# Seven block products in place of eight for 4 of 16 inner tiles of a gate/up projection

## The chip, the cores and the metric

The kernel runs on one core of a Trainium2 chip. Its time is the device time in microseconds; the kernel before takes 2282.24 us (median of 3 runs, 2281.66 to 2282.36).

## The reference

A decoder of two layers for 256 tokens of width 2048, in float32: layer 0 is gated linear attention, layer 1 stick-breaking attention, and behind each comes a SwiGLU feed-forward part of inner width 5632. The change is about the feed-forward part:

```python
def rmsnorm(x, w):
    xf = x.astype(jnp.float32)
    xf = xf * lax.rsqrt(jnp.mean(xf * xf, axis=-1, keepdims=True) + EPS)
    return xf.astype(x.dtype) * w

def swiglu(h, w_gate_up, w_down):
    gate, up = jnp.split(h @ w_gate_up, 2, axis=-1)
    return (jax.nn.silu(gate) * up) @ w_down

h = h + swiglu(rmsnorm(h, ffn_norm_w[layer]), ffn_w_gate_up[layer], ffn_w_down[layer])
```

## The kernel before

Every large product is done at a reduced float32 format of TensorE, with each operand split exactly into a high and a low part, and with three matmuls: high times high, high times low, low times high. `load_w` (L110) streams 128 x 1024 weights into `raw` (pool `wraw`, four buffers), ScalarE casts them to `hi` (L119), and VectorE subtracts to get `lo` (L120), in pool `wsp` of three buffers.

`gemm_tok` (L123) keeps 128 x 128 of the activations stationary and moves 512 columns of weights; for each of the inner tiles `k` and each of the two token tiles `t` it issues the three matmuls of L137. It accumulates in one PSUM bank per token tile, from pool `ps_acc` with four banks; two more pools, `ps_tr` and `ps_x`, have two banks each, for transposes and for the small products of the attention parts.

In `ffn` (L245) the 5632 inner columns are 11 blocks of 512, in three passes of four, four and three. For each block there is a `gemm_tok` over the 16 inner tiles for gate, one for up, and then an evacuation: Silu on ScalarE with the token's reciprocal rms as scale (L258), a product on VectorE (L261), four transposes for each token tile (L264), and the split into `hid_h` and `hid_l` (L267, L268). A pass ends with the down projection of its blocks, `residual_gemm` (L230), which adds to the residual `h` 512 columns at a time (L235).

The activations of a feed-forward part, `xh` and `xl`, are made ahead of it. While the output projection of the attention part runs, `norm_block` (L225) takes each 512 columns of `h` that are done, sums their squares (L202), transposes them (L194) and splits them times the norm's gain (L184, L185). They are not yet divided by the rms. It is known only once all four quarters are summed (`inv_rms`, with a power on POOL at L211), and is multiplied in by the evacuations, L258 and L261.

The transposed activations lie in pool `xt`, two buffers of 32 KB per partition; a feed-forward part uses one of them for `xh` and `xl`.

The order of the instructions on each engine isn't that of the text. A scheduler goes through them once, when the kernel is built, with the text's order as priority and a modelled time for each; each engine's queue is then fixed. A tile of a pool can be filled again once the last reader of the buffer is done.

Of the kernel before, what the change touches and what calls it, by code (L numbers as in the profile page):

```python
# [8 lines left out]
F32 = mybir.dt.float32  # L9
F32R = mybir.dt.float32r  # L10
# [28 lines left out]
PASSES = ((0, 1, 2, 3), (4, 5, 6, 7), (8, 9, 10))  # L39


@with_exitstack
def trunk_kernel(
# [67 lines left out]
    def load_w(ap, k0, nk, c0, ncol, dst=None):  # L111
# [7 lines left out]
        a.copy(hi[:, :n], raw[:, :n])  # L119
        v.tensor_tensor(lo[:, :n], raw[:, :n], hi.bitcast(F32)[:, :n], ALU.subtract)  # L120
# [21 lines left out]
    def gemm_tok_in_turn(w_ap, kt, lhs, c0, evac, k_row0):  # L142
        """gemm_tok with the block of weights held, so that the first token tile is done before the second."""
# [13 lines left out]
    def gemm_col(w_ap, c0, nct, xhl, dst, scale):  # L157
        """dst[column, 256 tokens] for nct column tiles from c0, times scale: weights stationary, activations moving."""
# [45 lines left out]
    def inv_rms(ss, n, name):  # L204
        """ss [P, NT, parts] -> (sum / n + eps) ** -0.5, [P, NT]"""
# [8 lines left out]
    def along_tokens(r, name):  # L214
        """r [token, NT] -> [P, 256], the same row on every partition."""
# [14 lines left out]
    def residual_gemm(w_ap, kt, lhs, k_row0, after=None, after_tile=None):  # L230
        """h += lhs @ w, 512 columns at a time."""
# [13 lines left out]
    def ffn(layer, xh, xl, r, **after):  # L245
        w_gu, w_dn = ffn_w_gate_up[layer], ffn_w_down[layer]
        lhs = lambda k, t: (xh[:, k, t * P : (t + 1) * P], xl[:, k, t * P : (t + 1) * P])
        with tc.tile_pool(name=f"ffn{layer}", bufs=2) as fp:
            for blocks in PASSES:
                hid = []  # L250
                for b in blocks:
# [3 lines left out]
                    sg = [fp.tile([P, NB], F32, name="sg", bufs=4) for _ in range(NT)]  # L255

                    def evac_gate(t, acc, sg=sg):
# [339 lines left out]
```

## Time and profile before

| | |
|---|---|
| median of the runs | 2282.24 us |
| profiled execution, first to last instruction (span) | 2279.7 us |
| what the median has beyond the span | 2.5 us |
| TensorE busy | 2263.7 us, 99% |
| VectorE busy | 1238.5 us, 54% |
| ScalarE busy | 1046.4 us, 46% |
| mean granted TensorE clock | 0.999 of full speed |

The profile is of one execution, and its own time is the span. Busy time of TensorE overlaps from one matmul to the next: a matmul has 0.39 us on its row and the next one begins before it ends, so what a matmul costs is read from the distance of starts. PE is TensorE's matmuls, PEld its weight loads, DVE is VectorE, ACT is ScalarE, SP the queue that issues the loads.

### The profile page before, as it was taken

The numbers are of one execution on the slowest core, as the hardware profiler recorded it, in microseconds if no ns is written. First come the engines' busy times: TensorE is split into PE (matmuls) and PEld (weight loads), VectorE is DVE, ScalarE is ACT, GpSimd is POOL, SyncE is SP. The second block draws the span as 40 slices with busy tenths as digits, with TensorE's granted clock in tenths as the row PEclk, the third lists the DMA queues.
The fourth block names the chain that finished last, engine by engine and source line by source line (L and its number), as shares of the span: only waits on it lengthen the run. The fifth ranks groups of instructions, "written<-read, shape, count | busy, mean of one in ns | idle before, by whom it ended". The sixth has DMA issues, their size and how long they took to land.

```text
span 2279.7 us, 27154 instructions
## 1 busy us (share of the span) xinstructions
PE 2263.7 (99%) x10658; PEld 1891.0 (83%) x10658; DVE 1238.5 (54%) x1251; ACT 1046.4 (46%) x1222; POOL 60.4 (3%) x72
## 2 busy tenths in 40 slices
PE   9999999999999999999999999999999999999998
PEld 7888878888888888888888888888888888888887
DVE  6766455545545545544664567655445444554555
ACT  6544444444434443344554446554444344434444
POOL 2100000000000000000000111000000000000000
PEclk9999999999999999999999999999999999999999
DMA  7554555666666666666566654556666666666664
GB/s 224 169 164 143 153 166 181 188 188 190 188 193 193 189 189 193 194 186 193 185 186 194 186 185 141 167 184 191 186 192 190 193 190 192 186 194 193 191 188 157
DMA packets 242712, 419.23 MB, mean 184 GB/s; under 512 B 12972, under 2 KB 64264, under 8 KB 242456
## 3 DMA queue, kind: packets, MB, share of 16 engines
q1 hardware_dynamic: 242408, 416.44, 60.5%
q8 instruction: 83, 1.36, 0.2%
q10 hardware_dynamic: 176, 1.06, 0.1%
q14 instruction: 45, 0.37, 0.0%
HBM read 415.35 MB, written 2.10 MB: 183 GB/s over the span
## 4 chain that ended last, share of the span: by engine, by line
PE 99%; DVE 0%; issue 0%; DMA 0%; ACT 0%; SPq 0%; POOLq 0%; POOL 0%; DVEq 0%; ACTq 0%
PE acc L137 82%; PE acc L169 7%; PE acc L170 4%; PE px L397 1%; PE tr L264 1%; PE tr L194 1%; PE acc L172 0%; PE acc L154 0%; PE px L494 0%; PE tr L525 0%; PE px L439 0%; DMA raw<-in_gla_w_in_dram 0%; DVE B L356 0%; PE px L409 0%; PE tr L526 0%
## 5 line engine op out<-in xcount | busy, mean ns | idle before, releaser
L120 DVE TENSOR_TENSOR lo<-raw,hi 128x1024 fp32r<-128x1024 f32 (+1 forms) x783 | 972.1, 1243 | 938.4 <-ACT hi L119 937.9
L119 ACT CAST hi<-raw 128x1024 fp32r<-128x1024 f32 (+1 forms) x783 | 823.7, 1052 | 1043.1 <-PE acc L137 904.3
L137 PE MATMUL acc<-hi,xhl 128*128 128x512 f32 x4096 | 1274.7, 391 | 0.8 <-ACT xhl L184 0.8
L137 PEld LDWEIGHTS acc<-hi,xhl 128*128 128x128 f32 x4096 | 769.4, 188 | 161.1 <-issue 1.9
L137 PE MATMUL acc<-lo,xhl 128*128 128x512 f32 x2048 | 799.9, 391 | 0.0
L137 PEld LDWEIGHTS acc<-lo,xhl 128*128 128x128 f32 x2048 | 385.1, 188 | 78.7
L137 PE MATMUL acc<-lo,hid_h 128*128 128x512 f32 x680 | 264.9, 390 | 0.0
L137 PE MATMUL acc<-hi,hid_l 128*128 128x512 f32 x680 | 264.6, 389 | 0.0
L169 PE MATMUL acc<-xhl,hi 128*128 128x512 f32 x735 | 256.1, 396 | 0.6 <-ACT hi L119 0.6
L137 PE MATMUL acc<-hi,hid_h 128*128 128x512 f32 x680 | 240.7, 390 | 0.0
L170 PE MATMUL acc<-xhl,lo 128*128 128x256 f32 x784 | 209.6, 281 | 2.1 <-DVE lo L120 2.0
L169 PEld LDWEIGHTS acc<-xhl,hi 128*128 128x128 f32 x735 | 134.8, 188 | 27.7 <-ACT hi L119 1.0
L170 PEld LDWEIGHTS acc<-xhl,lo 128*128 128x128 f32 x784 | 147.7, 189 | 8.8 <-DVE lo L120 3.0
L137 PEld LDWEIGHTS acc<-hi,hid_l 128*128 128x128 f32 x680 | 127.7, 188 | 26.5
L137 PEld LDWEIGHTS acc<-hi,hid_h 128*128 128x128 f32 x680 | 127.6, 188 | 26.3
L137 PEld LDWEIGHTS acc<-lo,hid_h 128*128 128x128 f32 x680 | 127.6, 188 | 26.1
L184 ACT ACTIVATE xhl<-tr,gains 128x256 fp32r<-128x256 f32 x96 | 40.9, 470 | 28.2 <-PE tr L194 20.9
L185 DVE SCALAR_TENSOR_TENSOR xhl<-tr,gains,xhl 128x256 fp32r<-128x256 f32 x96 | 42.4, 478 | 13.0 <-ACT xhl L184 13.0
L235 DVE TENSOR_TENSOR h<-acc,h 128x512 f32<-128x512 f32 x64 | 41.2, 682 | 7.6 <-PE acc L154 5.2
L258 ACT ACTIVATE sg<-acc,n_r 128x512 f32<-128x512 f32 x44 | 30.0, 690 | 20.8 <-PE acc L137 20.8
L267 ACT CAST hid_h<-tr 128x512 fp32r<-128x512 f32 x44 | 23.6, 589 | 31.4 <-PE tr L264 31.4
L268 DVE TENSOR_TENSOR hid_l<-tr,hid_h 128x512 fp32r<-128x512 f32 x44 | 28.3, 686 | 17.3 <-ACT hid_h L267 17.3
(153 smaller groups left out, 709.1 us busy)
## 6 DMA issues: line engine op xcount, KB each, us to landing
raw<-in_ffn_w_gate_up_dram SPq DMA_DIRECT2D x352, 512.0 KB, 3.9
raw<-in_ffn_w_down_dram SPq DMA_DIRECT2D x176, 512.0 KB, 3.7
raw<-in_gla_w_in_dram SPq DMA_DIRECT2D x97, 512.0 KB, 3.9
raw<-in_sb_w_kv_dram SPq DMA_DIRECT2D x64, 512.0 KB, 3.9
raw<-in_gla_w_out_dram SPq DMA_DIRECT2D x32, 512.0 KB, 3.7
raw<-in_sb_w_q_dram SPq DMA_DIRECT2D x32, 512.0 KB, 3.6
raw<-in_sb_w_out_dram SPq DMA_DIRECT2D x32, 512.0 KB, 3.7
h<-in_x_dram SPq DMA_DIRECT2D x8, 256.0 KB, 5.7
```

The costliest lines, as they stand in the source:

```text
L119: a.copy(hi[:, :n], raw[:, :n])
L120: v.tensor_tensor(lo[:, :n], raw[:, :n], hi.bitcast(F32)[:, :n], ALU.subtract)
L137: pe.matmul(acc[t], l, r[:, j, :], start=(k == 0 and n == 0), stop=(k == kt - 1 and n == 2))
L169: pe.matmul(acc[c], hi[:, j, cs], both, start=first, stop=False)
L170: pe.matmul(acc[c][:, :S], lo[:, j, cs], xhl[:, k0 + j, 0, :], start=False, stop=False)
L184: a.mul(dst_h, src, scale)
L185: v.scalar_tensor_tensor(dst_l, src, scale, dst_h.bitcast(F32), ALU.mult, ALU.subtract)
L194: pe.transpose(tp[:, o : o + P], src(t)[:, j * P : (j + 1) * P], ident)
L235: v.tensor_tensor(hs, acc, hs, ALU.add)
L258: a.activation(sg[t], acc, AF.Silu, scale=r[:, t : t + 1])
L267: a.copy(hh[:, :, ts], tv)
L268: v.tensor_tensor(hl[:, :, ts], tv, hh.bitcast(F32)[:, :, ts], ALU.subtract)
```

## The change

Four of the 16 inner tiles are taken as two pairs. For a pair, the two inner tiles, the two token tiles and the two column halves (gate, up) make a 2 x 2 by 2 x 2 block product. Done plainly it has eight block products; here it has seven, on sums and differences of blocks (Winograd's form of Strassen's scheme). The sums mix the two token tiles, so the tokens have to be divided by their rms ahead.

- `normed_xt`, at the start of `ffn`, replaces `norm_block` ahead of the two feed-forward parts: it waits for the rms, scales `h` by it (ScalarE, 512 columns and one token tile at a time), transposes and splits all four quarters, and forms and splits the sums of the token tiles for the two pairs. The output projection is followed only by the sums of squares (`sums`).
- Block 0 of each layer is done plainly (`eight`), with gate and up side by side. The ten others are done by `seven`: first four products M1, M5, M6, M7 over both pairs into four PSUM banks, then the recombination of the banks by ScalarE and VectorE, and then the three other products of each pair, onto the recombined banks, with two plain inner tiles behind each pair, and then the rest of the twelve plain tiles.
- The differences of weights are formed by VectorE in `room`, which is the second buffer of pool `xt`. They are split in a pool with two buffers (`pair(..., fp, bufs=2)`).
- A weight load takes one inner tile of gate and up together, where it took two inner tiles of one.
- `ps_acc` has six banks and `ps_x` is gone; its users take banks from `ps_acc`.
- The evacuations have no scale.

The diff, cut to its core:

```diff
+XS = 2
-    ps_acc = ctx.enter_context(tc.tile_pool(name="ps_acc", bufs=4, space=PSUM))
+    ps_acc = ctx.enter_context(tc.tile_pool(name="ps_acc", bufs=6, space=PSUM))
-    ps_x = ctx.enter_context(tc.tile_pool(name="ps_x", bufs=2, space=PSUM))
+    def split(hi, lo, src):
+        a.copy(hi, src)
+        v.tensor_tensor(lo, src, hi.bitcast(F32), ALU.subtract)
+    def three(acc, x, w, start, stop, onto=False):
+        (xh, xl), (wh, wl) = x, w
+        for n, (l, r) in enumerate(((xh, wh), (xh, wl), (xl, wh))):
+            pe.matmul(acc, l, r, start=start and n == 0, stop=stop and n == 2, skip_group_check=onto)
+    def normed_xt(ss, key, sums):
+        xh, xl, _ = xt_pair()
+        sh, sl = sums
+        r = inv_rms(ss, D, "n")
...
+        for nb in range(NCB):
+            hs = []
+            for t in range(NT):
+                n = stat.tile([P, NB], F32, name="junk")
+                a.mul(n, h[:, t, nb * NB : (nb + 1) * NB], r[:, t : t + 1])
+                hs.append(n)
+            make_xt(lambda t: hs[t], nb, [(key, 0, xh, xl)])
+        for i in range(XS):
+            q = stat.tile([P, 2, S], F32, name="junk")
+            v.tensor_tensor(q, xh.bitcast(F32)[:, 2 * i : 2 * i + 2, :], xl.bitcast(F32)[:, 2 * i : 2 * i + 2, :], ALU.add)
+            a11, a12, a21, a22 = (q[:, k, t * P : (t + 1) * P] for t in (0, 1) for k in (0, 1))
+            f = stat.tile([P, 4, P], F32, name="junk")
+            v.tensor_tensor(f[:, 0, :], a21, a22, ALU.add)
+            v.tensor_tensor(f[:, 1, :], f[:, 0, :], a11, ALU.subtract)
+            v.tensor_tensor(f[:, 2, :], a11, a21, ALU.subtract)
+            v.tensor_tensor(f[:, 3, :], a12, f[:, 1, :], ALU.subtract)
+            split(sh[:, i], sl[:, i], f)
+        return xh, xl
...
+            room = xt_pair()[2].bitcast(F32).rearrange("p k s c -> p (k s c)").rearrange("p (n c) -> p n c", c=NB)
...
+            def pair(src, pool, **kw):
+                hi, lo = (pool.tile([P, 1024], F32R, name=n, **kw).rearrange("p (k c) -> p k c", k=2) for n in ("hi", "lo"))
+                n = src.shape[1]
+                split(hi[:, :n], lo[:, :n], src)
+                return [(hi[:, j, :], lo[:, j, :]) for j in range(n)]
+            def plain(acc, b, k, start, stop, onto=False):
+                raw = wraw.tile([P, 1024], F32, name="raw").rearrange("p (k c) -> p k c", k=2)
+                load(raw, b, k)
+                for c, w in enumerate(pair(raw, wsp)):
+                    for t in range(NT):
+                        three(acc[t][c], lhs(k, t), w, start, stop, onto)
+            def seven(b):
+                m1, m5, m6, m7 = (ps_acc.tile([P, NB], F32, name="acc") for _ in range(4))
+                held = []
+                for i in range(XS):
+                    first, last = i == 0, i == XS - 1
+                    w3 = room[:, 3 * (i % 2) : 3 * (i % 2) + 3, :]
+                    t32 = room[:, 6 + 2 * (i % 2) : 8 + 2 * (i % 2), :]
+                    w2 = room[:, 10 + 3 * i : 13 + 3 * i, :]
+                    load(w3[:, 0:2, :], b, 2 * i)
+                    load(w2[:, 0:2, :], b, 2 * i + 1)
+                    v.tensor_tensor(w3[:, 2, :], w3[:, 1, :], w3[:, 0, :], ALU.subtract)
+                    b11, t1 = pair(w3[:, 0::2, :], fp, bufs=2)
+                    v.tensor_tensor(t32, w2[:, 1:2, :].broadcast_to([P, 2, NB]), w3[:, 1:3, :], ALU.subtract)
+                    v.tensor_tensor(w2[:, 2, :], w2[:, 0, :], t32[:, 1, :], ALU.subtract)
+                    t3, t2 = pair(t32, fp, bufs=2)
+                    three(m1, lhs(2 * i, 0), b11, first, last)
+                    three(m5, summed(i, 1), t1, first, last)
+                    three(m6, summed(i, 2), t2, first, last)
+                    three(m7, summed(i, 3), t3, first, last)
+                    held.append(w2)
+                p1, p5, u2 = (fp.tile([P, NB], F32, name="part", bufs=3) for _ in range(3))
+                a.copy(p1, m1)
+                a.copy(p5, m5)
+                v.tensor_tensor(u2, m6, p1, ALU.add)
+                v.tensor_tensor(m6, u2, p5, ALU.add)
+                v.tensor_tensor(m7, m7, u2, ALU.add)
+                v.tensor_tensor(m5, m7, p5, ALU.add)
+                acc = ((m1, m6), (m7, m5))
+                todo = list(range(2 * XS, KD))
+                for i, w2 in enumerate(held):
+                    b21, b22 = pair(w2[:, 0:2, :], wsp)
+                    (t4,) = pair(w2[:, 2:3, :], wsp)
+                    three(m1, lhs(2 * i + 1, 0), b21, False, False, True)
+                    three(m6, summed(i, 4), b22, False, False, True)
+                    three(m7, lhs(2 * i + 1, 1), t4, False, False, True)
+                    for _ in range(2):
+                        plain(acc, b, todo.pop(0), False, False, True)
...
+                    acc = seven(b) if b else eight(b)
+                    for t, (gate, up) in enumerate(acc):
+                        sg = fp.tile([P, NB], F32, name="sg", bufs=3)
+                        a.activation(sg, gate, AF.Silu)
+                        v.tensor_tensor(sg, up, sg, ALU.mult)
...
-    residual_gemm(gla_w_out[0], KD, lhs_of(oh, ol), 0, lambda nb, ss=ss: norm_block(ss, nb, [("ffn0", 0, fh, fl)]))
-    r1 = inv_rms(ss, D, "n")
+    residual_gemm(gla_w_out[0], KD, lhs_of(oh, ol), 0, sums(ss))
+    ffn(0, ss, "ffn0", after=to_kqv)
```

## Rows read from the trace of the kernel before

**Rows 1.** Part 1 of the page: busy us (share of the span) xinstructions of each engine.

```profile
PE 2263.7 (99%) x10658; PEld 1891.0 (83%) x10658; DVE 1238.5 (54%) x1251; ACT 1046.4 (46%) x1222; POOL 60.4 (3%) x72
```

**Rows 2.** Part 4: the chain of waits that ended last, shares by engine.

```profile
PE 99%; DVE 0%; issue 0%; DMA 0%; ACT 0%; SPq 0%; POOLq 0%; POOL 0%; DVEq 0%; ACTq 0%
```

**Rows 3.** That chain in order of time, two gate/up blocks: start, us, what.

```profile
474.98 43.54 PE acc L137 x192
519.39 43.54 PE acc L137 x192
```

**Rows 4.** TensorE's waits, two of five: line <- releaser: us, times, longest.

```profile
PE tr L104 <- POOL mf L327: 3.8, 1, 3.8
...
PE acc L170 <- DVE lo L120: 2.0, 1, 2.0
```

**Rows 5.** Waits of VectorE and ScalarE, the largest of each.

```profile
DVE lo L120 <- ACT hi L119: 937.9, 732, 3.3
...
ACT hi L119 <- PE acc L137: 904.3, 553, 3.8
```

**Rows 6.** Busy us of PE, PEld, DVE, ACT, POOL in one block; PEclk, DMA share, GB/s.

```profile
475.20:519.60 44.40, 44.40 (x202) 36.85 (x201) 22.21 (x20) 19.19 (x21) 0.00 (x0) 1.00 0.64 190
```

**Rows 7.** Timeline, output projection to layer 0's first gate tiles: start, us, engine, line, operation.

```profile
424.47 1.28 DVE L235 TENSOR_TENSOR h<-acc,h 128x512 f32<-128x512 f32 x2
...
424.53 0.84 PE L137 MATMUL acc<-hi,xhl 128*128 128x512 f32 x3
...
427.72 0.69 POOL L211 TENSOR_TENSOR n_r<-n_s,neg_half 128x2 f32<-128x2 f32 x1 [87.07 <-DVE n_s L209]
...
429.52 0.38 PE L194 MATMUL tr<-ident,h 128*128 128x128 f32 x2
...
429.98 0.82 PE L194 MATMUL tr<-ident,h 128*128 128x128 f32 x6
...
430.50 0.84 ACT L184 ACTIVATE xhl<-tr,gains 128x256 fp32r<-128x256 f32 x2 [1.73 <-PE tr L194]
```

**Rows 8.** Groups by line and shape: xcount | busy us, mean ns | idle before.

```profile
L120 DVE TENSOR_TENSOR lo<-raw,hi 128x1024 fp32r<-128x1024 f32 x781 | 970.7, 1244 | 935.7 <-ACT hi L119 935.2
...
L119 ACT CAST hi<-raw 128x1024 fp32r<-128x1024 f32 x781 | 822.4, 1053 | 1042.5 <-PE acc L137 904.3 <-PE acc L169 98.8 <-ACT xhl L184 17.1
...
L551 DVE TENSOR_TENSOR h<-h,fw 128x512 f32<-128x512 f32 x6 | 3.9, 686 | 0.2 <-ACT junk L202 0.2
...
L484 ACT ACTIVATE vv<-acc,n_r 128x512 f32<-128x512 f32 x8 | 5.4, 690 | 4.0 <-PE acc L137 4.0
...
L558 ACT ACTIVATE h<-h,y_r 128x512 f32<-128x512 f32 x2 | 1.4, 723 | 2.1 <-POOL y_r L211 2.1
...
L268 DVE TENSOR_TENSOR hid_l<-tr,hid_h 128x512 fp32r<-128x512 f32 x44 | 28.3, 686 | 17.3 <-ACT hid_h L267 17.3
```

**Rows 9.** Windows (columns of rows 6) with and behind idle TensorE.

```profile
66.00:70.00 4.00, 2.03 (x13) 1.46 (x12) 4.00 (x7) 1.67 (x3) 0.00 (x0) 1.00 0.03 11
...
2270.00:2272.00 2.00, 1.32 (x6) 0.75 (x4) 0.64 (x1) 0.00 (x0) 0.00 (x0) 1.00 0.28 109
...
2274.00:2276.00 2.00, 0.00 (x0) 0.00 (x0) 1.45 (x3) 0.63 (x1) 0.00 (x0) 1.00 0.37 139
...
2276.00:2278.00 2.00, 0.00 (x0) 0.00 (x0) 0.00 (x0) 0.00 (x0) 0.00 (x0) 0.65 1.02 381
```

**Rows 10.** Timeline at the end of a gate/up block.

```profile
513.30 1.41 DVE L261 SCALAR_TENSOR_TENSOR sg<-acc,n_r,sg 128x512 f32<-128x512 f32 x2
...
518.36 1.03 PE L264 MATMUL tr<-ident,sg 128*128 128x128 f32 x8
...
519.61 1.29 DVE L268 TENSOR_TENSOR hid_l<-tr,hid_h 128x512 fp32r<-128x512 f32 x2 [0.79 <-ACT hid_h L267]
```

**Rows 11.** Timeline of TensorE around its wait for a low part.

```profile
67.02 0.63 PE L169 MATMUL acc<-xhl,hi 128*128 128x512 f32 x2
69.61 0.50 PE L170 MATMUL acc<-xhl,lo 128*128 128x256 f32 x2 [1.97 <-DVE lo L120]
```

More of the change, by code (lines that the diff above doesn't have):

```diff
@@ new lines, in ffn, with load, eight @@
+    def ffn(layer, ss, key, **after):
+        w_gu, w_dn = ffn_w_gate_up[layer].rearrange("k (g c) -> k g c", g=2), ffn_w_down[layer]
+        with tc.tile_pool(name=f"ffn{layer}", bufs=2) as fp:
+            sh, sl = (fp.tile([P, XS, 4, P], F32R, name=n, bufs=1) for n in ("sum_h", "sum_l"))
+            xh, xl = normed_xt(ss, key, (sh, sl))
+            lhs = lambda k, t: (xh[:, k, t * P : (t + 1) * P], xl[:, k, t * P : (t + 1) * P])
+            summed = lambda i, n: (sh[:, i, n - 1, :], sl[:, i, n - 1, :])
+            room = xt_pair()[2].bitcast(F32).rearrange("p k s c -> p (k s c)").rearrange("p (n c) -> p n c", c=NB)
+            def load(dst, b, k):
+                nc.sync.dma_start(dst, w_gu[k * P : (k + 1) * P, :, b * NB : (b + 1) * NB])
+            def pair(src, pool, **kw):
[46 more added lines that the diff above has]
+                        plain(acc, b, todo.pop(0), False, False, True)
+                while todo:
+                    k = todo.pop(0)
+                    plain(acc, b, k, False, not todo, True)
+                return acc
+            def eight(b):
+                acc = [[ps_acc.tile([P, NB], F32, name="acc") for _ in (0, 1)] for _ in range(NT)]
+                for k in range(KD):
+                    plain(acc, b, k, k == 0, k == KD - 1)
+                return acc
@@ L342, in trunk_kernel @@
         for k0 in range(0, GKT, 2):
-            up = ps_x.tile([P, 512], F32, name="px")
+            up = ps_acc.tile([P, 512], F32, name="acc")
             for j in (0, 1):
@@ L384, in level @@
             if m == P:
-                sp = ps_x.tile([P, 512], F32, name="px")
+                sp = ps_acc.tile([P, 512], F32, name="acc")
                 for hd in range(GH):
@@ L391, in level @@
             if m:
-                sp = ps_x.tile([P, 512], F32, name="px")
+                sp = ps_acc.tile([P, 512], F32, name="acc")
                 for x8 in range(GH * NT):
@@ L404, in level @@
             for h0 in (0, 2):
-                sp = ps_x.tile([P, 512], F32, name="px")
+                sp = ps_acc.tile([P, 512], F32, name="acc")
                 for x4 in range(4):
@@ L447, in trunk_kernel, with sums, after, to_kqv @@
     lhs_of = lambda xh, xl: (lambda k, t: (xh[:, k, t * P : (t + 1) * P], xl[:, k, t * P : (t + 1) * P]))
-    fh, fl, _ = xt_pair()
-    ss = stat.tile([P, NT, NCB], F32, name="ss")
-    residual_gemm(gla_w_out[0], KD, lhs_of(oh, ol), 0, lambda nb, ss=ss: norm_block(ss, nb, [("ffn0", 0, fh, fl)]))
-    r1 = inv_rms(ss, D, "n")
-    kh, kl, khl = xt_pair()
-    qh, ql, qhl = xt_pair()
-    ss = stat.tile([P, NT, NCB], F32, name="ss")
-    ffn(0, fh, fl, r1, after=lambda nb, ss=ss: norm_block(ss, nb, [("kv", 0, kh, kl), ("attn1", 0, qh, ql)]))
+    def sums(ss):
+        def after(nb):
+            for t in range(NT):
+                sumsq(ss[:, t, nb : nb + 1], h[:, t, nb * NB : (nb + 1) * NB])
+        return after
+    ss = stat.tile([P, NT, NCB], F32, name="ss")
+    residual_gemm(gla_w_out[0], KD, lhs_of(oh, ol), 0, sums(ss))
+    kqv = []
+    def to_kqv(nb):
+        if not kqv:
+            kqv.extend((xt_pair(), xt_pair(), stat.tile([P, NT, NCB], F32, name="ss")))
+        (kh, kl, _), (qh, ql, _), ss = kqv
+        norm_block(ss, nb, [("kv", 0, kh, kl), ("attn1", 0, qh, ql)])
+    ffn(0, ss, "ffn0", after=to_kqv)
+    (kh, kl, khl), (qh, ql, qhl), ss = kqv
     r2 = inv_rms(ss, D, "n")
@@ L534, in trunk_kernel @@
             attend(pr, qp)
-    fh, fl, _ = xt_pair()
-    ss = stat.tile([P, NT, NCB], F32, name="ss")
-    residual_gemm(sb_w_out[0], KD, lhs_of(oh, ol), 0, lambda nb, ss=ss: norm_block(ss, nb, [("ffn1", 0, fh, fl)]))
-    r3 = inv_rms(ss, D, "n")
+    sf = stat.tile([P, NT, NCB], F32, name="ss")
+    residual_gemm(sb_w_out[0], KD, lhs_of(oh, ol), 0, sums(sf))
     ss = stat.tile([P, NT, NCB], F32, name="ss")
```

27 lines of the change are left out of this document (8 added, 19 removed).

## The prediction

> **What bounds the kernel now.** The page's first part comes first: TensorE is busy 99% of the span, VectorE 54%, ScalarE 46% [rows 1]. A busy TensorE need not be its peak, so the chain that ended last is next: 99% of it is TensorE [rows 2]. In order of time that chain shows the gate/up blocks as unbroken runs of 192 matmuls in 43.54 us, so one 512-column matmul takes 43.54 / 192 = 0.2268 us, and the next run begins 44.41 us after the last [rows 3]; the 0.87 us between are eight transposes. The waits say whether anything feeds it late: TensorE's waits are five rows, 7.5 us in all, of which the two largest are shown [rows 4]. The other side waits for TensorE: ScalarE's weight cast stands 904 us for matmuls, and VectorE's subtraction follows the cast [rows 5]. So matmuls taken out of gate/up are worth their 0.2268 us, as long as the two engines that split the weights keep up. In one gate/up block they are busy 22.2 and 19.2 us of 44.4 [rows 6].
>
> **The matmuls removed.** A block has 16 inner tiles x 2 token tiles x 2 (gate, up) x 3 (split products) = 192 matmuls. In a seven-product block four inner tiles are taken in two pairs; a pair needs 7 products in place of 8, 3 matmuls each, so 6 fewer per block. Ten of a layer's 11 blocks are changed: 2 x 10 x 6 = 120 matmuls, 120 x 0.2268 = 27.2 us off the path. Everything else has to stay under that.
>
> **The start of each feed-forward layer.** Now the transposes of the residual need no scale, so three quarters of them lie beside the output projection and the last 512 columns beside the first gate tiles. After the change the tokens are divided first, so no transpose can begin before the last square is summed. The chain from the trace of layer 0 [rows 7]: the projection's last matmul is the first of the three that begin at 424.53, so TensorE's next slot is 424.76. The residual add of both token tiles ends at 425.75, the squares, the reduction and the scalar follow, and the POOL power ends at 427.72 + 0.69 = 428.41. All that is there today, under matmuls. New behind it: two ScalarE scalings (0.72 each by the scaling from SBUF, 0.69 by that from PSUM [rows 8]) to 429.85; four transposes, half of the 1.03 for eight [rows 10], to 430.4; the first split (0.84 for two, so 0.42) to 430.85; and the first gate matmul at about 430.95. The hole is 430.95 - 424.76 = 6.2 us, less 0.87 for eight transposes that are in the stream today: 5.3 us, and twice that is 10.6 us. If fewer casts stand between, 4.5 each; if two casts of 1.05 get in, 7.4. The other three quarters are covered by block 0, which stays with eight products: each asks ScalarE for 2 x 0.72 + 4 x 0.42 + 4 casts x 1.05 = 7.3 us in the 10.9 us of its 48 matmuls.
>
> **The clock in that hole.** This trace has two stretches to compare. Ahead of 69.6 TensorE stood for 2 us [rows 11] and the granted clock stayed at 1.00, its 2.4 GHz level; after its last matmul, which ended at about 2271.3, it was still 1.00 up to 2276 and 0.65 on average over the next 2 us, so (0.6 us at 1.00, 1.4 at 0.50) it fell to the 1.2 GHz level at about 2276.6, 5.3 us after [rows 9]. A hole of 6.2 us with four transposes late in it lies at that edge. I take 0.5 us per layer, 1 us in all; the ends are 0 and 3.1 per layer (as long at half speed as the hole was, 6.2 us of which half is lost). The Trainium skill speaks against this edit: "TensorE: Matmul & The Clock Gate", section "Why this matters for your kernels", asks for no long idle gaps between bursts of matmuls, since one puts the array back to its half clock. By the rule the upper end is due, by the row at 67 us nothing; it is a rival below.
>
> **The first part of a seven-product block.** Per pair VectorE makes three differences (0.69 + 1.24 + 0.69 by the rows for 512 and 1024 columns in rows 8) and two subtractions for the split (2 x 1.24): 5.1 us, against 12 matmuls of 2.72 us. The differences need only loaded weights and their own room, free since early in the block before, so they lie under that block, where VectorE is half idle. The splits can't go so far ahead: their pool holds two buffers, and the first pair takes both. With the block's first matmul at 0: the buffer with B11 and T1 is last read by the sixth matmul, which ends at 5 x 0.2268 + 0.39 = 1.52; cast 1.05 and subtraction 1.24 [rows 8] make the low part ready at 3.9, and TensorE wants it at 2.95. A hole of 0.95. What fills it: the high-part matmul of the next product, 0.23, and the eight transposes of the block before, 0.87, which today stand 3.7 us after that block's last evacuation [rows 10], just where the hole is. That the order is made by readiness and not by the text is seen where two high-part matmuls stand ahead of a low part that is late [rows 11]. In 16 blocks 1.10 of filling covers 0.95; in the four that open a pass behind a down projection (blocks 4 and 8) there are no such transposes, and 0.72 stays open. The second buffer's split (ready at about 5.2) is in time.
>
> **The recombination.** VectorE needs two operations (0.69 each, by the subtraction from PSUM in rows 8) behind M6's last matmul before M6's bank can be added to, 1.4 us, plus the matmul's 0.39. Meanwhile TensorE has M7 (0.68), the product on M1 (0.68) and the first plain tile's part on M1 (0.68): 2.04 us. Covered, if taken in this order. The two copies on ScalarE end earlier.
>
> **What crowds VectorE.** In the ten microseconds from the end of a block it has the two gate times up (1.4), one plain subtraction (1.24), two of the pair (2.5), two for the hidden tile (1.37) and the four of the recombination (2.75): 9.3 us, so an awkward order costs. For the block: 22.2 + 5.2 (differences) + 3.9 (two and two half subtractions more) + 2.7 = 34 us of 43; ScalarE 19.2 + 4.7 = 24. I take 0.4 us per block for 16 and 0.75 for four, 9.4 us in all. The ends: 0, and 1.9 (the hole of 0.95 unfilled, and as much again when the recombination waits behind both hidden subtractions), 38 us over 20 blocks.
>
> **Edits put at nothing.** The evacuations without scale are no longer than today's. The sums of token tiles, some 3 us of VectorE per pair, lie under block 0. Loads move the same bytes in the same 512 KB, and DMA is at 0.64 there [rows 6]. One PSUM pool of six in place of four and two: outside the feed-forward TensorE waits under 4 us for what could change, so within 3 us either way.
>
> **Sum.** -27.2 + 10.6 + 1.0 + 9.4 = -6.2 us on the profiled span of 2279.7, so 2273.5; the median of the runs is 2282.24, 2.5 above that span, so 2276.0.
>
> **Rivals.**
> (a) The first part fills completely: no stall in a block, start holes of 4.5: -27.2 + 9 = -18, 2264. For it: TensorE hardly waits anywhere today. Against: VectorE has never been asked for 34 of 43 us in the part of the trace that shows blocks.
> (b) The other side: the two buffers of the pair's splits decide. Place: the second pair and the recombination of each changed block. The point from which it decides is a stall of (27.2 - 11.6) / 20 = 0.78 us a block. Price at 1.5 us a block: -27.2 + 11.6 + 30 = +14.4, 2297. For it: 5.1 us of VectorE against 2.72, and a hole of 0.95 that something else must fill. Against: the filling is there in 16 of 20 blocks.
> (c) The first layer's order is worse: all 32 transposes ahead of the first gate matmul. Then the hole grows by three quarters of 2 x 0.72 + 4 x 0.42 = 3.1 us, about 9.4 a layer: -6.2 + 18.8 = +12.6, 2295. Against: transposes and matmuls mix in twos and sixes in today's order [rows 7].
> (d) The half clock: it falls in both holes and costs 3.1 each: -6.2 - 1 + 6.2 = -1, 2281. For it: the fall at the end of the trace, and the rule named above. Against: transposes come inside the hole.
> (e) That the product count doesn't matter, because the splits set the pace: ScalarE's 904 us of waiting for matmuls excludes it for plain tiles; for the changed part it is (b).
>
> **How the numbers follow.** About 0.2%, 4.6 us, can be told from no change. Forecast (2268 to 2282): 0.42; (a) 0.15; (b) 0.25; (c) 0.08; (d) 0.10. Faster by more: all of (a), 0.35 of the forecast's and 0.03 of (d), so 0.53. Within: 0.07 of the forecast, 0.07 of (d), 0.04 of (b) at its lower edge, so 0.18. Slower: the rest of (b), and (c), 0.29. The range goes from (a) to beyond (b) at 1.5 us a block: 2264 to 2300; the forecast's own is 2268 to 2282.
>
> **What would show it.** TensorE's matmuls fall by 120. After each output projection a hole of about 6 us with squares, POOL power and scalings in it, and the granted clock there says whether (d) holds. From run to run a block takes 43.05 us plus its stall, in place of 44.41; the waits of TensorE for VectorE's low part and for the banks of the recombination give that stall, and over 0.78 us a block decides for (b). VectorE's busy time should rise by about 20 x 11.8 = 236 us. The prediction is wrong if blocks are no shorter than 44.4 us, or if the holes are over 8 us.

## The result: 4.2% slower, and the profile after

The changed kernel takes 2376.6 us (2373.9 to 2384.1) beside 2281.9 for the one before: ratio 1.042, 95% interval 1.0404 to 1.0437. Forecast were 2276.0 and a range of 2264 to 2300, so sign and range were both wrong. Ratios leave out disturbed executions; there is one, of the four of e2 below, at 5058.7 us, without which e2's median would be 2343.3 and not 2344.1. Parts 1 and 4 of its page answer to [rows 1, 2]:

```profile
PE 2288.5 (96%) x10538; PEld 1878.5 (79%) x10538; DVE 1448.8 (61%) x1555; ACT 1131.7 (48%) x1362; POOL 54.6 (2%) x72
...
PE 80%; DVE 9%; DMA 6%; issue 2%; ACT 1%; POOL 1%; SPq 0%; DVEq 0%; POOLq 0%; ACTq 0%
```

The 120 matmuls are gone, and VectorE's busy time rose by 210 us, where 236 were forecast. Yet TensorE, 99% of the chain before, is 80% of it now, and VectorE has 9% with an average load of only 61%. TensorE's waits (line, releaser: us in total, times, longest) stand against 7.5 us in five rows before [rows 4]:

```profile
PE acc L253 <- DVE lo L113: 26.1, 35, 1.2
PE acc L604 <- POOL qp L180: 11.1, 8, 2.3
PE acc L253 <- DVE acc L331: 9.8, 6, 2.2
PE tr L198 <- ACT junk L265: 8.6, 2, 4.3
PE acc L488 <- DVE lev L480: 4.6, 1, 4.6
PE acc L253 <- ACT hi L112: 4.4, 11, 1.1
...
PE acc L447 <- POOL gl L180: 3.6, 1, 3.6
```

Three places can be read off. L253 is gate/up (low parts, recombination). L604, L488 and L447 are not in the feed-forward at all: attention, the scores and the log decay of layer 0. L198 is the start of each feed-forward layer. By the last residual additions of each stage, the span grew by 9.1 us up to the first output projection, 35.8 and 34.7 in the two feed-forward layers and 17.4 in attention.

One seven-product block (columns as in [rows 6]) took 46.5 us, not 43.05 plus a little, with VectorE at 32 us, close to the 34 forecast:

```profile
820.00:866.50 46.50, 44.56 (x196) 35.33 (x195) 31.97 (x35) 22.88 (x27) 0.00 (x0) 1.00 0.60 181
```

Of the 3.45 us beyond 43.05, TensorE was idle for 1.94 (46.50 - 44.56). The rest lies in its busy time, where matmuls begin further apart; so the rows of waits show less than what the stops cost. VectorE is not full in a block; it is full at the handover from one block to the next. VectorE's timeline there (start, us, line, operation; in brackets the idle time before and what ended it):

```profile
772.19 1.23 DVE L319 TENSOR_TENSOR xhl<-xhl 128x1024 f32<-128x1024 f32 x1 [1.36 <-DMA xhl<-in_ffn_w_gate_up_dram]
773.33 0.68 DVE L365 TENSOR_TENSOR sg<-acc,sg 128x512 f32<-128x512 f32 x1
773.93 1.22 DVE L113 TENSOR_TENSOR lo<-raw,hi 128x1024 fp32r<-128x1024 f32 x1
775.06 0.69 DVE L320 TENSOR_TENSOR xhl<-xhl 128x512 f32<-128x512 f32 x1
775.66 0.69 DVE L330 TENSOR_TENSOR part<-acc,part 128x512 f32<-128x512 f32 x1
776.26 1.22 DVE L113 TENSOR_TENSOR lo<-xhl,hi 128x1024 fp32r<-128x1024 f32 x1
777.39 0.70 DVE L331 TENSOR_TENSOR acc<-part 128x512 f32<-128x512 f32 x1
778.00 0.70 DVE L332 TENSOR_TENSOR acc<-acc,part 128x512 f32<-128x512 f32 x1
```

From 772.19 to 786.2 VectorE has no idle time. L319 and L320 are differences of the second pair. The first of them waited 1.36 us for its load, and the gate times up (L365) stood behind it in VectorE's queue. In the chain of waits (start, us, what) that load begins when a subtraction of a held tile of the block before ends:

```profile
766.16 1.24 DVE lo L113
767.41 4.75 DMA xhl<-in_ffn_w_gate_up_dram
```

Over the whole run VectorE stood 58.3 us for loads ahead of a difference (13.5 ahead of L317, 44.8 ahead of L319). The two differences then stand ahead of the plain low part, the recombination (L330 to L333) and the low parts of held tiles. TensorE's timeline in the same stretch stops for those:

```profile
775.20 0.50 PE L253 MATMUL acc<-lo,xhl 128*128 128x512 f32 x1 [0.21 <-DVE lo L113]
...
777.53 0.50 PE L253 MATMUL acc<-lo,xhl 128*128 128x512 f32 x1 [1.14 <-DVE lo L113]
...
780.81 1.36 PE L253 MATMUL acc<-hi,xhl 128*128 128x512 f32 x3 [0.21 <-ACT hi L112]
```

### The profile page after: what moved, and what is told of

Same layout as the page of the kernel before. It is cut to its first block, busy times and chain, and to the rows that moved or that the text cites. A ratio compares the mean times of both kernels' runs of the same rounds, so it can differ in the third digit from the quotient of the medians.

```text
span 2376.7 us, 27301 instructions
## 1 busy us (share of the span) xinstructions
PE 2288.5 (96%) x10538; PEld 1878.5 (79%) x10538; DVE 1448.8 (61%) x1555; ACT 1131.7 (48%) x1362; POOL 54.6 (2%) x72
## 4 chain that ended last, share of the span: by engine, by line
PE 80%; DVE 9%; DMA 6%; issue 2%; ACT 1%; POOL 1%; SPq 0%; DVEq 0%; POOLq 0%; ACTq 0%
PE acc L141 36%; PE acc L253 28%; PE acc L173 7%; DMA xhl<-in_ffn_w_gate_up_dram 6%; DVE lo L113 5%; PE acc L174 4%; PE acc L497 1%; ACT hi L112 1%; PE tr L198 1%; DVE hid_l L113 1%; DVE part L330 0%; PE acc L604 0%; POOL qp L180 0%; DVE xhl L320 0%; PE acc L176 0%
## 5 line engine op out<-in xcount | busy, mean ns | idle before, releaser
L113 DVE TENSOR_TENSOR lo<-raw,hi 128x1024 fp32r<-128x1024 f32 (+1 forms) x703 | 874.8, 1246 | 700.5 <-ACT hi L112 699.9
L112 ACT CAST hi<-raw 128x1024 fp32r<-128x1024 f32 (+1 forms) x703 | 735.3, 1049 | 870.6 <-PE acc L141 424.7
L253 PE MATMUL acc<-hi,xhl 128*128 128x512 f32 x2416 | 775.4, 396 | 6.2 <-ACT hi L112 4.4
L253 PEld LDWEIGHTS acc<-hi,xhl 128*128 128x128 f32 x2416 | 457.4, 190 | 114.2 <-ACT hi L112 13.4
L253 PE MATMUL acc<-lo,xhl 128*128 128x512 f32 x1208 | 478.9, 397 | 26.1 <-DVE lo L113 25.6
L141 PE MATMUL acc<-hi,xhl 128*128 128x512 f32 x1280 | 402.7, 393 | 0.9 <-ACT xhl L188 0.9
L253 PEld LDWEIGHTS acc<-lo,xhl 128*128 128x128 f32 x1208 | 229.2, 190 | 86.9 <-DVE lo L113 41.1
L141 PEld LDWEIGHTS acc<-hi,xhl 128*128 128x128 f32 x1280 | 240.5, 188 | 52.3 <-issue 1.7
L141 PE MATMUL acc<-lo,xhl 128*128 128x512 f32 x640 | 251.7, 394 | 0.0
L112 ACT CAST hi<-xhl 128x1024 fp32r<-128x1024 f32 (+1 forms) x160 | 149.5, 945 | 181.6 <-PE acc L253 156.1
L113 DVE TENSOR_TENSOR lo<-xhl,hi 128x1024 fp32r<-128x1024 f32 (+1 forms) x160 | 172.2, 1089 | 50.9 <-ACT hi L112 50.6
L141 PEld LDWEIGHTS acc<-lo,xhl 128*128 128x128 f32 x640 | 120.5, 188 | 26.3 <-issue 1.9
```

Source lines behind the costliest of these rows:

```text
L112: a.copy(hi, src)
L113: v.tensor_tensor(lo, src, hi.bitcast(F32), ALU.subtract)
L141: pe.matmul(acc[t], l, r[:, j, :], start=(k == 0 and n == 0), stop=(k == kt - 1 and n == 2))
L253: pe.matmul(acc, l, r, start=start and n == 0, stop=stop and n == 2, skip_group_check=onto)
```

## Experiments: which part costs what

All times are medians, and the kernel before took 2281.8 to 2282.0 beside each. The theory, from the waits above: the shared PSUM pool costs 26.5 us, the divided tokens 16 to 20, and the rest is stalls in seven-product blocks. The rivals were the prediction's own sizes and, for e4, the new shape of a block.

**e1_one_pool**: the kernel before with the pools alone changed.

```diff
-    ps_acc = ctx.enter_context(tc.tile_pool(name="ps_acc", bufs=4, space=PSUM))
-    ps_x = ctx.enter_context(tc.tile_pool(name="ps_x", bufs=2, space=PSUM))
+    ps_acc = ctx.enter_context(tc.tile_pool(name="ps_acc", bufs=6, space=PSUM))
...
-            za = ps_x.tile([P, 512], F32, name="px")
+            za = ps_acc.tile([P, 512], F32, name="acc")
```

> The kernel before with one edit: PSUM pool of six banks that the small products of the two attention parts share, in place of four and two. Theory: the 9.1 us that the GLA part and the 17.4 us that the attention part of layer 1 are longer in the changed kernel's trace come from the shared pool alone, so 2282 + 26.5 = 2308 us, with the feed-forward parts as long as before (732 and 722 us). Rival, as the prediction put it: the pool is worth at most 3 us either way, so 2279 to 2285, and the two parts are longer in the changed kernel because the scheduler's order there is moved by the feed-forward parts next to them.

2315.4, ratio 1.0148 (1.0132 to 1.0163): +33.6, where the theory had 26.5 and the rival at most 3. The same waits as in the changed kernel appear in a kernel with nothing else changed:

```profile
PE acc L493 <- POOL qp L175: 13.0, 8, 2.3
PE acc L387 <- DVE lev L379: 4.6, 1, 4.6
...
PE acc L346 <- POOL gl L175: 3.6, 1, 3.6
```

L493 is a score's matmul that waits until POOL has scaled the queries, once for each of the eight pairs of heads. Before, it took its bank from a pool of its own, and the next pair's query product ran meanwhile.

**e2_scoped**: the changed kernel with banks 4+2 outside the feed-forward and 6 in it.

```diff
+    share(0, 4, 2)
...
+    share(1, 6, 0)
     ffn(0, ss, "ffn0", after=to_kqv)
+    share(2, 4, 2)
...
-            za = ps_acc.tile([P, 512], F32, name="acc")
+            za = banks["x"].tile([P, 512], F32, name="px")
```

> The changed kernel with its PSUM split by part: four and two banks in the GLA and attention parts as before, six in the feed-forward parts as in the change. Theory (the pool costs 26.5 us outside the feed-forward parts): 2376.6 - 26.5 = 2350 us, GLA and attention parts back to 424.5 and 386 us. Rival (the pool is not it): 2374 to 2379 us.

2344.1, ratio 1.0265 (1.0248 to 1.0282): 32.5 less than the changed kernel. The pool's price is nearly the same added (33.6) or taken away.

**e11_text_order**: e1 with the next pair's query product written ahead of the scores.

```diff
-            attend(pr, qp)
+            if ahead is not None:
+                attend(pr - 1, ahead)
+            ahead = qp
+        attend(SH // 2 - 1, ahead)
```

> The kernel with one PSUM pool of six and nothing else changed (2315.35 us), with the text of the attention part in another order: the query product of the next pair of heads is written ahead of the attention of this pair. Theory F (a pool hands out its banks in the order of the text, so the next query product gets no bank until the scores of this pair have theirs, and these wait for POOL's scaling): the attention part goes from 406 to 386 to 390 us, 2296 to 2300 us. Rival (six shared banks are simply too few for both): it stays over 400 us, 2310 to 2320.

2299.1, ratio 1.0075 (1.0061 to 1.0089): 16.2 of the 33.6 come back, and layer 1's attention takes 386.7 us beside 385.9 before and 405.7 in e1. So in layer 1 the price is one of order: one pool gave its banks out in the order of the text, and the next query product stood behind the scores in it. The rest is in layer 0, where the text was left as it was.

**e3_normed**: the kernel before with the tokens divided ahead of their split.

```diff
+                a.mul(n, h[:, t, nb * NB : (nb + 1) * NB], r[:, t : t + 1])
...
-                        a.activation(sg[t], acc, AF.Silu, scale=r[:, t : t + 1])
+                        a.activation(sg[t], acc, AF.Silu)
```

> The kernel before with one edit: the tokens are divided by their rms ahead of transposing and splitting, at the start of each feed-forward part; blocks, products and PSUM as before. Theory from the changed kernel's trace (TensorE stands 6.5 us, of which 0.87 is transposes that stood there before, and the next nine matmuls are 0.43 us apart in place of 0.23, so 2.5 us with the transposes at the same rate): 2 x 8.2 = 16 us, so 2298 us. Rival, the prediction's own term: 2 x 5.8 = 11.6 us, so 2293.5. Second rival: the later quarters also stall TensorE (block 0 ended 9.9 us later in the changed kernel, not 8.2): 20 us, 2302.

2297.0, ratio 1.0066 (1.0049 to 1.0083): +15.2, where the prediction had 11.6. TensorE's timeline in the changed kernel at the start of layer 0's feed-forward answers to [rows 7]:

```profile
433.69 0.39 PE L141 MATMUL acc<-hi,xhl 128*128 128x512 f32 x1
438.37 2.16 PE L198 MATMUL tr<-ident,junk 128*128 128x128 f32 x8 [4.29 <-ACT junk L265]
440.45 0.80 PE L253 MATMUL acc<-hi,xhl 128*128 128x512 f32 x1
...
444.03 1.46 PE L253 MATMUL acc<-hi,xhl 128*128 128x512 f32 x5
```

and the windows of its end and of what follows to [rows 9]:

```profile
438.00:441.00 3.00, 2.63 (x9) 1.94 (x10) 0.48 (x1) 1.99 (x4) 0.00 (x0) 0.50 0.93 324
441.00:444.00 3.00, 3.00 (x8) 2.32 (x7) 1.96 (x4) 2.22 (x6) 0.00 (x0) 0.50 1.00 356
```

The hole is 440.45 - 433.92 = 6.5 us, where 6.2 were forecast. But behind it the granted clock is 0.50, the 1.2 GHz level: eight matmuls take 444.03 - 440.45 = 3.58 us in place of 1.81. So a start costs 6.5 - 0.87 + 1.77 = 7.4, two of them 14.9. The eight transposes in the hole ran at 0.50 as well, in 2.16 us where eight took 1.03 before [rows 10]. By that some 1.1 us of the hole are the clock's too, an estimate, and 2.9 of a start in all.

**e4_all_eight**: the changed kernel with `eight()` for every block.

```diff
-                    acc = seven(b) if b else eight(b)
+                    acc = eight(b)
```

> The changed kernel with all eleven blocks done as eight products (gate and up side by side in four banks, loads of one inner tile of both), no differences, no recombination; sums of tokens are still formed but not used. Theory (the seven-product blocks themselves cost the rest): blocks go back to 44.4 us, so 2282 + 26.5 for the pool + 16 to 20 for the starts = 2325 to 2329 us, 50 us under the changed kernel. Rival: the new shape of a block (side by side, evacuation of four banks at its end, loads of one inner tile) is what costs 2 to 5 us a block: 2360 to 2376 us.

2331.4, ratio 1.0214 (1.0199 to 1.0230), which is 33.6 + 15.2 + 0.7 above before: the new shape of a block (gate and up together, six banks) costs nothing that these runs show. Thus the seven-product blocks alone make the changed kernel 2376.6 - 2331.4 = 45.2 us slower although they hold 27.2 us less of matmuls: 72 us of stalls, 3.6 per block where 0.4 to 0.75 were forecast. The rows of waits above show 40 of the 72 (26.1 + 9.8 + 4.4).

## Experiments: why a seven-product block stalls

In the expectations V is VectorE's added work, B the two buffers for a pair's splits, and D the chain through the room (load, difference, split). All start from e2 (2344.1).

**e5_no_differences**: tiles as loaded in place of differences, so the products are not the reference's.

```diff
-                    v.tensor_tensor(w3[:, 2, :], w3[:, 1, :], w3[:, 0, :], ALU.subtract)
-                    b11, t1 = pair(w3[:, 0::2, :], fp, bufs=2)
...
+                    b11, t1 = pair(w3[:, 0:2, :], fp, bufs=2)
...
```

> The changed kernel with its banks split by part (2344.1 us), and without VectorE's three differences of weights per pair; the raw weight tiles stand in for them, so the seven products are of other operands and the output is not the reference's. Loads, splits, matmuls and recombination are all still there. Theory V (VectorE is asked for some 14 us without a break where one block hands over to the next, and TensorE's 3.3 us of stall per block are its lateness): 5.2 us of VectorE per block go, most of them in that stretch, so 2 to 3 us a block, 2285 to 2305 us. Theory B (the two buffers of the pairs' splits set it): the splits come no earlier, 2335 to 2345 us.

2280.5, ratio 0.9994 (0.9984 to 1.0004): 63.6 less, a little below V's range. TensorE's waits for gate/up shrink to

```profile
PE acc L261 <- ACT hi L120: 2.4, 3, 1.1
...
PE acc L261 <- DVE lo L121: 1.8, 8, 0.3
```

With the differences gone, what stays above -27.2 and e3's +15.2 is 2280.5 - 2281.9 + 27.2 - 15.2 = 10.6 us, about the 9.4 that the prediction gave to all stalls. It had sized splits and recombination; in the blocks, the differences at their place are what it missed.

**e6_pool_differences**: the differences on POOL (`g.tensor_tensor` for `v.tensor_tensor` in three lines).

> The same base (2344.1 us) with the three differences per pair on POOL in place of VectorE. POOL's two-input operations of 512 columns took 1.3 to 2.0 us in the kernel before, so 10 to 16 us per block of 46, on an engine that does nothing else there. Theory V: VectorE is free of 5.2 us, but t32 and t1 come about 1 to 2 us later than on VectorE: 2300 to 2325 us. Theory D (what is late is the load of the held half of a pair, because its room is read up to the block's end): the chain from the load to the split gets longer, 2344 to 2370 us. Theory B: no change, 2335 to 2345.

2308.2, ratio 1.0115 (1.0099 to 1.0131): 36 less although each difference takes longer (1.8 and 2.8 us on POOL, 0.69 and 1.23 on VectorE). D, a chain that becomes longer, would have made it slower. A reason why it isn't the whole 63.6 stands in the last section.

**e7_third_room**: a third place for the held half of a pair.

```diff
+            spare, turn = fp.tile([P, 3, NB], F32, name="spare", bufs=1), [0]
...
-                    w2 = room[:, 10 + 3 * i : 13 + 3 * i, :]
+                    w2 = spare if turn[0] % 3 == 2 else room[:, 10 + 3 * (turn[0] % 3) : 13 + 3 * (turn[0] % 3), :]
```

> The same base (2344.1 us) with a third room for the held half of a pair, so that its load for the next block doesn't wait for this block's last read of it (the final gain vector moves into the free activation buffer to make space). Theory D: loads land 5 us or more earlier and the differences move out of the crowded stretch: 1 to 2 us a block, 2304 to 2324 us. Theories V and B: VectorE has the same work in the same order and the splits the same buffers, 2335 to 2345 us.

2347.8, ratio 1.0288 (1.0272 to 1.0305): nothing gained. The chain of waits of the changed kernel, which shows load, difference and low part one behind the other, had suggested D. But the third room didn't bring the loads earlier: VectorE stood 53.2 us for loads ahead of differences, beside 55.1 in e2. So e7 doesn't show what timely loads would be worth; that the chain's length isn't the main cost is shown by e6 and e12.

**e8_three_splits**: three buffers for the splits.

```diff
-                    b11, t1 = pair(w3[:, 0::2, :], fp, bufs=2)
+                    b11, t1 = pair(w3[:, 0::2, :], fp, bufs=3)
...
```

> The same base (2344.1 us) with three buffers in place of two for the splits of the pairs (the final gain vector moved as well). Theory B: a split can be made one step ahead, TensorE's waits for the low parts (2.0 of 3.3 us per block) go: 2300 to 2315 us. Theories V and D: the splits are late because VectorE or the load is, 2335 to 2345 us.

2326.8, ratio 1.0194 (1.0178 to 1.0210): 17 less, between the two expectations. TensorE's wait for low parts fell from 23.8 to 6.2 us, but that for M6's recombination rose from 9.5 to 22.5. (The final norm's gain vector moved as well, as in e7, e10 and e15; in e7 nothing was gained by it.)

**e9_divide_late** and **e10_divide_late_three_splits**: e6 with the division put back to the evacuation, then with three split buffers as well.

```diff
-                        a.activation(sg, gate, AF.Silu)
+                        a.activation(sg, gate, AF.Silu, scale=r[:, t : t + 1])
...
```

> The changed kernel with its banks split by part, the differences on POOL (2308.2 us as that) and the division by the rms put back behind the products: the sums of token tiles are formed of undivided tokens, as the products are linear in each token and the evacuation scales each token tile as in the kernel before. Theory (the starts of the feed-forward parts cost what the divided tokens alone cost, 15.2 us): 2293 us, TensorE's wait for the scaled tokens gone. Rival (the starts are hidden behind something else now that the blocks stall): over 2300.

> The same with three buffers for the splits of the pairs. If the gains add up (36 us for POOL, 17 us for the third buffer, 15.2 us for the late division off 2344.1): 2276 us, under the kernel before by 6. If the third buffer helps only against the lateness that POOL has already taken away: 2288 to 2293 us.

2303.8, ratio 1.0098 (1.0084 to 1.0111), and 2316.0, ratio 1.0162 (1.0141 to 1.0182). e9 missed its theory and lies where its rival put it, over 2300: 4.4 of 15.2 us came back. e10 missed both expectations: the third buffer cost 12 where it had gained 17. TensorE waits longer for single low parts, up to 4.0 us. In these runs effects measured one at a time did not add while the order of VectorE's work was left to come out as it may.

**e12_unread_differences**: e2's differences at full size, into room that no split reads; the splits as in e5. Against e5, with an unchanged line between the first and the second:

```diff
+                    v.tensor_tensor(w3[:, 2, :], w3[:, 1, :], w3[:, 0, :], ALU.subtract)
...
+                    v.tensor_tensor(t32, w2[:, 1:2, :].broadcast_to([P, 2, NB]), w3[:, 1:3, :], ALU.subtract)
+                    v.tensor_tensor(w2[:, 2, :], w2[:, 0, :], t32[:, 1, :], ALU.subtract)
```

> The kernel of e2_scoped with all its VectorE differences at their full sizes, but written to room that nothing reads; the splits read loaded tiles as in e5_no_differences (so the output isn't the reference's). VectorE is exactly as busy as in e2 (2344), and the chain load, difference, cast, subtraction is as short as in e5 (2280.5). If VectorE's occupancy is what costs (an in-order engine with ready work queued ahead of what TensorE wants): 2325 to 2345. If it is the length of the chain in front of each pair's split: 2280 to 2295. In between, both have a share, read off as (time - 2280.5) / 63.6 for the occupancy.

2333.1, ratio 1.0221 (1.0204 to 1.0238). The differences in VectorE's queue are (2333.1 - 2280.5) / 63.6 = 83% of it; that other work waits for their results is the smaller part. A place in the queue is more than the work done there: the differences still wait for loads in e12, and VectorE stood 28.8 us ahead of them. e12 doesn't part the one from the other.

**e13_differences_mid_block**: the next block's loads and differences written ahead of inner tile 10 of this block, and kept there by a call that fixes an instruction's place in the order.

```diff
+                    if k == 10:
+                        prepare(b + 1)
...
+                    tc.keep_in_program_order(v.tensor_tensor(w3[:, 2, :], w3[:, 1, :], w3[:, 0, :], ALU.subtract))
```

> The kernel of e2_scoped (2344) with the same loads and the same six VectorE differences, but those of the next block written into the middle of this block (ahead of inner tile 10) and kept there in the order of instructions, so that none stands at the handover between two blocks. VectorE's work is the same to the instruction. If it is its order at the handover that costs, nearly all of the 63.6 us that leaving the differences out gave comes back: 2282 to 2297, block period 43.2 to 43.8. If any 5.2 us more of VectorE per block cost TensorE (mean load, whatever the place): 2330 to 2345. If the kept instructions hold up loads or casts mid-block: in between, with a new wait for a low part near tile 10.

2292.5, ratio 1.0046 (1.0031 to 1.0061): 51.6 less with the same 1555 instructions on VectorE. So it is the place of the differences, with that of their loads, and not the work they are. VectorE no longer stands for a load ahead of any difference. No low part is late in gate/up any more; the only large wait left there is

```profile
PE acc L261 <- DVE acc L348: 17.0, 16, 1.1
```

**e14_mid_block_divide_late**: e13 with the division at the evacuation.

> e13 with the division put back to the evacuation. If the terms add: e13 less the 15.2 us that the division ahead cost (e3), so 2267 to 2282, which would be at or below the kernel before (2281.9). If late division costs VectorE or the handover something in this shape, as it did beside the differences on POOL (e9 gave only 4.4 of 15.2): 4 to 8 us below e13.

2281.5, ratio 0.9996 (0.9986 to 1.0005): 11.1 less, at the upper end of what was expected if the terms add. TensorE's timeline shows the stop that is left, in 16 of 20 blocks:

```profile
832.13 0.39 PE L261 MATMUL acc<-lo,sum_h 128*128 128x512 f32 x1
832.36 0.39 PE L261 MATMUL acc<-hi,sum_l 128*128 128x512 f32 x1
833.81 0.51 PE L261 MATMUL acc<-hi,sum_h 128*128 128x512 f32 x1 [1.06 <-DVE acc L336]
```

The second pair's products on M6 and M7 come last, behind M1's own additions, and what stands behind them in TensorE's queue adds to a bank that is still being recombined. That the two split buffers put them so late is the reading that e15 tests.

**e15_mid_block_three_splits**: e14 with the third buffer of e8.

> e14 (2281.5) with three buffers in place of two for the splits of a pair (the final norm's weight moves to a room that is free by then, as in e8). e14's trace leaves one stall per block: TensorE waits 1.1 us, 16 times, 17.3 us in all, for the second recombination, because the second pair's products on M6 and M7 come last, behind M1's own additions. With the third buffer the second pair is split a product earlier, both pairs' products on M6 and M7 come ahead of the transposes and of M1's addition, and 2.9 us of other matmuls lie between M6's last product and its first addition in place of 1.4. If that wait was the recombination's (the place decides): blocks of 43.1 to 43.4 us and 2258 to 2268, faster than the kernel before (2282.0). If the third buffer pulls VectorE's subtractions into the handover, as it did in e8 and e10: the wait turns into one for a low part, 2275 to 2300.

2257.8, ratio 0.9895 (0.9879 to 0.9912): 1.05% faster than the kernel before, the only version that is. None of TensorE's rows of waits is of gate/up (the two largest are shown), and TensorE works through a whole block while VectorE is as loaded as in the changed kernel:

```profile
PE tr L112 <- DMA gains_a<-in_attn_norm_w_dram: 3.7, 1, 3.7
PE acc L182 <- DVE lo L121: 2.0, 1, 2.0
```

```profile
780.00:823.10 43.10, 43.10 (x195) 35.78 (x195) 32.55 (x35) 23.17 (x26) 0.00 (x0) 1.00 0.64 196
```

VectorE's timeline at a handover of the same pass as in the first section has no difference in it, and the recombination (L335 to L338) follows the plain low part directly:

```profile
819.21 1.23 DVE L121 TENSOR_TENSOR lo<-raw,hi 128x1024 fp32r<-128x1024 f32 x1
820.35 0.69 DVE L335 TENSOR_TENSOR part<-acc,part 128x512 f32<-128x512 f32 x1
821.07 0.70 DVE L336 TENSOR_TENSOR acc<-part 128x512 f32<-128x512 f32 x1
821.68 0.69 DVE L337 TENSOR_TENSOR acc<-acc,part 128x512 f32<-128x512 f32 x1
822.58 0.69 DVE L121 TENSOR_TENSOR hid_l<-tr,hid_h 128x512 fp32r<-128x512 f32 x1 [0.21 <-ACT hid_h L120]
823.18 0.69 DVE L338 TENSOR_TENSOR acc<-acc,part 128x512 f32<-128x512 f32 x1
```

The third buffer, worth 17 in e8 and -12 in e10, is worth 23.6 here; the stop of 1.1 us is gone.

## Why the prediction was wrong

| term | forecast, us | measured, us | from |
|---|---|---|---|
| 120 matmuls | -27.2 | -27.2 by count; e15 is 24.0 below the kernel before | rows 3, e15 |
| two starts of a layer, with the clock | +11.6 | +15.2 | e3 |
| stalls in 20 blocks | +9.4 | +72 | after less e4, + 27.2 |
| one PSUM pool | within 3 | +33.6 | e1 (32.5 by e2) |
| sum | -6.2 | +94 (result +94.7) | |

**The failed step, first:** "The differences need only loaded weights and their own room, free since early in the block before, so they lie under that block, where VectorE is half idle." Readiness was taken for place. They did not lie in the idle half: they stand at the handover, in VectorE's fixed queue, ahead of the low parts and the recombination for which TensorE stops. Nor were they ready early: the load for the difference at 772.19 began at 767.41, when a held tile's subtraction had ended, 3.6 us ahead of the new block's first product at 771.00, and VectorE stood for it. A third room alone (e7) didn't bring the loads earlier; what else held them back stays open. The prediction listed 9.3 us of VectorE in those ten microseconds and saw that "an awkward order costs", but left the differences out of the list and took 0.4 us a block; 3.6 came. e5 (without them), e12 (unread) and e13 (moved) show it three ways. Its 34 of 43 us was a sound mean load, and e15 shows that load is harmless.

**The failed step, second:** "outside the feed-forward TensorE waits under 4 us for what could change, so within 3 us either way". A wait that isn't there before says nothing of what hides it. The two banks of `ps_x` were what let scores run inside the next query product; in one pool their order is the text's.

**The starts** were right in mechanism and off in size. The hole was 6.5 us for 6.2, though eight transposes and not four stand in it, at the half clock. The clock's fall, set at 0.5 a layer, cost 1.77 behind the hole and some 1.1 inside it. The end of the trace before had shown the clock falling 5.3 us after the last matmul [rows 9], so the upper side was the nearer row. Rival (d) was right in kind and, with 2.9 for its 3.1, nearly in size.

**Rival (b)** had the sign: 3.6 us a block came, far over its break-even of 0.78 (0.6 with the starts as measured). Its cause, the two split buffers, was the smaller part: a third was worth 17 us in e8 and 23.6 in e15, beside the 51.6 of e13. Its place, "the second pair and the recombination", is the wait that was left in e14. (a)'s 2264 was in reach of the same products: e15, which orders them otherwise and, dividing late, has no holes at the starts, passes it by 6. (c) didn't come: eight transposes, not 32, stand ahead of the first gate matmul. (e) is excluded by e15, which keeps 24.0 of the 27.2 us.

Open is what of e13's gain belongs to the differences' own time at the handover and what to VectorE standing for their late loads, which moved with them: no run brings the loads early and leaves the differences where they were.

## What to carry to other kernels

When work is added to an engine that others wait for, ask where in its queue it will stand at the moment when most is due, and whether what it reads will have landed by then, not whether its mean load leaves room; here 5.2 us a block cost 3.2 at the handover and at most 0.6 in mid-block (e13 beside e5). Pools are part of the order: merging two lets the text decide who gets a bank, and should be priced by the overlap that the second pool made possible. Fix the order first and judge buffers after, since the same third buffer was worth 17, -12 and 23.6 us under three orders.

## What the hardware showed that was not expected

**VectorE's subtractions take longer beside POOL.** In e9 a subtraction of 1.23 us took 3.44 while POOL worked; VectorE's timeline, then POOL's:

```profile
480.79 3.44 DVE L121 TENSOR_TENSOR lo<-raw,hi 128x1024 fp32r<-128x1024 f32 x1
```

```profile
480.75 2.39 POOL L315 TENSOR_TENSOR xhl<-xhl 128x1024 f32<-128x1024 f32 x1 [21.98 <-DVE sg L361]
```

It is longer by 2.2 us, nearly POOL's 2.39. The groups by shape in e2, then in e6 (count | busy us, mean ns | idle before):

```profile
L121 DVE TENSOR_TENSOR lo<-raw,hi 128x1024 fp32r<-128x1024 f32 x701 | 871.7, 1246 | 674.9 <-ACT hi L120 674.3
L121 DVE TENSOR_TENSOR lo<-xhl,hi 128x1024 fp32r<-128x1024 f32 x120 | 146.2, 1221 | 30.9 <-ACT hi L120 30.4
L121 DVE TENSOR_TENSOR hid_l<-tr,hid_h 128x512 fp32r<-128x512 f32 x44 | 28.5, 687 | 5.2 <-ACT hid_h L120 5.2
```

```profile
L121 DVE TENSOR_TENSOR lo<-raw,hi 128x1024 fp32r<-128x1024 f32 x701 | 927.5, 1329 | 653.8 <-ACT hi L120 653.0
L121 DVE TENSOR_TENSOR lo<-xhl,hi 128x1024 fp32r<-128x1024 f32 x120 | 166.0, 1395 | 56.0 <-ACT hi L120 55.6
L121 DVE TENSOR_TENSOR hid_l<-tr,hid_h 128x512 fp32r<-128x512 f32 x44 | 28.4, 681 | 5.1 <-ACT hid_h L120 5.1
```

Subtractions with both inputs in SBUF became longer on average, by 55.8 + 19.8 us in these two rows; those with one input from PSUM (`tr`) did not. The Trainium skill, "SBUF — State Buffer", section "Who interferes with whom", says that a VectorE instruction with two SBUF inputs contends with a GpSimd instruction that reads SBUF, since its second input comes through a read interface that they share. These rows agree. The addition that finishes M6 (`acc<-part`, both inputs in SBUF) went from 696 to 1535 ns. It is a likely reason why e6 got only 36 of the 63.6 us and perhaps why e9 and e10 missed; neither was tried apart.

**A stop costs more than it lasts.** In e1 TensorE waits 4.6 us once in layer 0's scores. The windows of the wait and of what follows (columns as in [rows 6]):

```profile
141.00:145.70 4.70, 0.13 (x2) 0.04 (x1) 3.97 (x5) 1.47 (x3) 1.26 (x1) 0.86 0.43 122
145.70:150.00 4.30, 4.30 (x21) 4.30 (x21) 1.50 (x2) 0.00 (x0) 0.00 (x0) 0.50 0.35 121
...
156.00:160.00 4.00, 4.00 (x15) 3.22 (x15) 3.80 (x3) 0.02 (x1) 0.00 (x0) 0.75 0.00 0
```

TensorE is busy from 145.7 on, but at 0.50, the 1.2 GHz level, to about 158: by estimate some 12 us that would have been 6 at 2.4 GHz. Before, the same stretch has 1.00 throughout, with TensorE busy in all of 140 to 260. e1's new waits sum to 13.0 + 4.6 + 3.6 = 21.2 us and its time to 33.6; this is about half of the difference.

The blocks pay this too. One window of the changed kernel:

```profile
592.00:600.00 8.00, 6.01 (x18) 4.06 (x19) 7.38 (x11) 2.23 (x3) 0.00 (x0) 0.79 0.46 132
```

Seven windows of 8 us in its gate/up blocks have 0.79. That makes 7 x 8 x 0.21 = 12 of the 72 us of stalls, an estimate. Over the whole profiled run its mean granted clock was 0.988, beside 0.999 before and 0.998 in e15.
